# A convolution with max pooling: eight row sums moved to accumulating DMA, two more steps row-transformed, and the order written anew

## The chip, the cores and the metric

The kernel runs on one core of one Trainium2 chip. The metric is the device time of one execution in microseconds (us). The engines are named as in the profile: PE is TensorE (matrix products), PEld its loading of weights, DVE is VectorE, ACT is ScalarE, POOL is GpSimd, SP is SyncE, which here only issues transfers. Each engine works through its own list of instructions in order. It waits on semaphores for what other engines or transfers have to deliver, and whatever stands behind a waiting instruction on its list waits too.

## What is computed

A 3 x 3 convolution with zero padding over 16 images of 64 x 64 pixels and 64 channels, to 128 channels, and then the maximum over each 2 x 2 block of pixels:

```python
batch, c_in, h, w, c_out, k = 16, 64, 64, 64, 128, 3
x_pad = np.pad(x, ((0, 0), (0, 0), (1, 1), (1, 1)))
conv[b, co] += weight[co, ci, kh, kw] * x_pad[b, ci, kh:kh+h, kw:kw+w]   # over ci, kh, kw
output[b, co, i, j] = np.max(conv[b, co, 2*i:2*i+2, 2*j:2*j+2])
```

x, weight and the output are float32; the products are made in bfloat16 and summed in float32.

## The kernel before, in words

**Tiling.** Two images lie in the 128 partitions at a time (64 channels each), so there are eight pairs of images. A pair is cut into four quarters of 16 rows. One quarter of one pair is a step; there are 32 steps, 0 to 31. A step makes 8 rows of output for each of its two images, and its products run in two lanes, one per image (h = 0 or 1), each of which contracts over 64 partitions. Every product is three instructions (one per column of the 3 x 3 window) over 8 rows of 64 columns, at line 200. Products of the two lanes are issued in turn, so that two run at once.

**Two kinds of steps.** The string TYPES says of each step whether it is of kind K or W. Both need only sums and differences of the two rows that the pooling joins.

- A K step loads its rows as bfloat16 by a casting transfer from GpSimd's queue (`kload`, L95, tile `kx`), and adds each even row to the odd row after it on VectorE (KS, L298, tile `ks`). It makes five products per lane: PA1, PA2, PB1, PB2 and PR. That is 30 product instructions per step.
- A W step loads its rows as float32 by SP's queue (`wload`, L106, tile `wx`, of which there are three, each for a whole pair). From `wx` it makes three bfloat16 operands by row: E, the difference within each pair of rows (L329, tile `we`, 128 x 512); D, the differences to the rows above and below (L338, tile `wd`, 128 x 1024, always on GpSimd); and WS, the sum within each pair of rows (tile `ws`, 128 x 512). It makes four products per lane: P2 on `we`, P0 and P3 on `wd`, P1 on `ws`. That is 24 product instructions per step.

E runs on GpSimd, or on VectorE for the steps in DIFF_ON_VECTOR. WS runs on VectorE in one of two forms: a reduction (L312, for the steps in SUM_BY_REDUCTION) or a plain addition (L320). A GpSimd operation on SBUF is made to wait for the latest VectorE operation of that kind that stands ahead of it in the order (`behind`); the reductions are not counted among these.

**After the products.** Each lane of a step has two accumulators, a and b, out of eight banks of PSUM. EV on ScalarE copies a out to SBUF (L396, or L398 with a change of sign in a W step). In a W step, SE on ScalarE also copies a into b as a start (L408). MX on VectorE takes the larger of b and the copy (L424); the last product is then added to b; OD on ScalarE copies the odd columns out (L428); CM on VectorE takes the larger of even and odd columns (L434), and the result is stored through SP (L444; half of the last step through ScalarE's queue).

**Order.** All is written out by hand in one list, ORDER, with no scheduler behind it. An entry such as `P2.14.1` is product P2 of step 14 in lane 1, `L.14` the load of step 14, `LK.1.0` a load for K steps, `E.14`, `D.14`, `WS.14` the operands. The place of an entry sets its place on its engine. An entry of a product is issued only when the other lane has one too. At the start the weights are combined (D2, D0, GM, GP), turned by TensorE (T...) and copied out (V...), and the first steps of either kind run in halves (F and G). The pairs of images are given out to the K steps first, and then to the W steps.

Before, 11 steps are K and 21 are W; four E are on VectorE and 16 on GpSimd (the first W step makes its own in halves, L350 and L365); 11 WS are reductions and 10 plain additions.

Of the kernel before, what the change touches and what calls it, by code (L numbers as in the profile page):

```python
# [11 lines left out]
def kernel(  # L12
# [21 lines left out]
    R = HO // NQ  # L34


    TYPES = "KWKWWKWKWWKWWKWKWWKWWKWWWWKWWKWW"
    DIFF_ON_VECTOR = (3, 4, 6, 11,)
    CAST_ON_VECTOR = ()
    SUM_BY_REDUCTION = (1, 3, 9, 11, 12, 14, 16, 17, 19, 20, 22,)  # L40
    N = len(TYPES)
    KSTEPS = [s for s in range(N) if TYPES[s] == "K"]
    WSTEPS = [s for s in range(N) if TYPES[s] == "W"]
# [3 lines left out]

    const = ctx.enter_context(tc.tile_pool(name="const", bufs=1))
    kx_pool = ctx.enter_context(tc.tile_pool(name="kx_pool", bufs=-(-NK // NQ)))
    d_pool = ctx.enter_context(tc.tile_pool(name="d_pool", bufs=5))  # L50
    e_pool = ctx.enter_context(tc.tile_pool(name="e_pool", bufs=5))
    ws_pool = ctx.enter_context(tc.tile_pool(name="ws_pool", bufs=5))
    ks_pool = ctx.enter_context(tc.tile_pool(name="ks_pool", bufs=4))
    ev_pool = ctx.enter_context(tc.tile_pool(name="ev_pool", bufs=7))
    od_pool = ctx.enter_context(tc.tile_pool(name="od_pool", bufs=6))
    o_pool = ctx.enter_context(tc.tile_pool(name="o_pool", bufs=6))
    psum = ctx.enter_context(tc.tile_pool(name="psum", bufs=1, space=bass.MemoryType.PSUM))

# [10 lines left out]
    def behind(inst, other):  # L69
        if other is not None:  # L70
            tc.add_manual_dep(inst.ins, other.ins.name, SYNC, reason="order")
# [231 lines left out]
    def wx_rows(s):  # L303
        p, q = place[s]
        return wx[p % NWX], 2 * R * q + 1

    def ws(s):
        row["ws", s] = ws_pool.tile([128, R, W], BF16, name="ws")
        t, f = wx_rows(s)
        if s in SUM_BY_REDUCTION:  # L310
            with nc.allow_low_precision("bf16 operand of TensorE, as the other row sums"):
                nc.vector.tensor_reduce(  # L312
                    out=row["ws", s],
                    in_=t[:, f : f + 2 * R, :].rearrange("p (r two) w -> p r w two", two=2),
                    axis=mybir.AxisListType.X,
                    op=ADD,
                )
            return
        on_vector(
            nc.vector.tensor_tensor(  # L320
                out=row["ws", s], in0=t[:, f : f + 2 * R : 2, :], in1=t[:, f + 1 : f + 2 * R : 2, :], op=ADD
            )
        )
# [62 lines left out]

    def late_load(s):
        behind(wload(s), sbuf_op[0])

    ev, od, ot, made = {}, {}, {}, {}  # L390

# [58 lines left out]
    def cast_more(first):  # L450
# [36 lines left out]
    for m in PRODUCTS:  # L487
        steps[m] = lambda s, h, m=m: product(m, s, h)

    ORDER = """  # L490
        D0 g2 g1 TD0 TG2 g0 D2 XEa PR.0.1 TD2 VG2 PA1.2.1 VD0 TG0 uG1 TG1 GS F.2.0 VD2 XOa LB.3 LB.4 LB.6
        LB.8 LB.9 GM VG0 F.3.0 XOb F.0.0 uGM F.1.0 VG1 F.0.1 TGM PA2.2.1 XEb LK.0.0 F.1.1 F.2.1 F.3.1 VGM GP
        Ea KS.0 Eb EV.0.1 G.0.0 EV.0.0 G.0.1 uGP P2.3.1 SEa.0 SEa.1 SEb.1 MX.0.1 Da Db TGP SEb.0 MX.0.0 VGP
        LK.0.1 X2 PR.0.0 G.1.0 X1 G.2.0 PB1.2.1 PB2.2.1 WS.1 G.2.1 G.1.1 L.11 P0.3.1 PA1.2.0 PA2.2.0 P3.3.1
        OD.0.0 OD.0.1 EV.1.0 KS.2 E.3 CM.0.1 EV.1.1 P1.1.1 D.3 CM.0.0 PR.2.1 PB1.2.0 P2.3.0 MX.1.0 PB2.2.0
        EV.2.1 P1.3.1 SE.3.1 EV.2.0 WS.3 MX.1.1 P1.1.0 SE.3.0 P0.3.0 MX.2.0 MX.2.1 EV.3.1 PR.2.0 EV.3.0 D.4
        MX.3.1 OD.2.0 PA1.5.1 OD.1.0 E.4 PA1.5.0 PA2.5.0 P3.3.0 OD.1.1 OD.2.1 L.12 L.14 PA2.5.1 OD.3.1
        P2.4.1 CM.1.1 CM.2.0 P2.4.0 CM.1.0 PA1.7.1 D.6 EV.5.0 CM.3.1 CM.2.1 MX.3.0 PA2.7.1 PB1.5.1 SE.4.0
        PA1.7.0 PA2.7.0 EV.5.1 SE.4.1 EV.7.0 PB2.5.1 P0.4.1 P0.4.0 P2.6.1 KS.7 E.6 P3.4.1 WS.4 WS.6 P1.3.0
        EV.4.0 PR.5.1 KS.5 WS.8 EV.7.1 P0.6.1 PB1.5.0 PB1.7.0 PB2.5.0 PB2.7.0 L.16 P1.4.1 EV.4.1 MX.5.1  # L500
        P3.4.0 OD.3.0 SE.6.1 MX.5.0 LK.1.0 LK.1.1 CM.3.0 MX.4.1 P3.6.1 OD.5.1 PB1.7.1 MX.7.0 PB2.7.1 PR.5.0
        OD.5.0 P2.6.0 EV.6.1 E.8 PR.7.0 MX.4.0 OD.4.1 OD.7.0 CM.5.1 D.8 P1.4.0 SE.6.0 OD.4.0 CM.5.0 E.9
        MX.6.1 CM.7.0 CM.4.0 P1.6.1 P2.8.0 CM.4.1 D.9 P2.8.1 SE.8.0 P0.6.0 P2.9.1 MX.7.1 P3.6.0 OD.6.1
        EV.6.0 P0.8.0 L.17 P3.8.0 SE.8.1 CM.6.1 PR.7.1 EV.8.0 OD.7.1 P0.8.1 MX.6.0 SE.9.1 E.11 MX.8.0 P1.6.0
        D.11 CM.7.1 P2.9.0 OD.6.0 EV.8.1 CM.6.0 WS.9 P3.8.1 P1.8.0 P0.9.1 PA1.10.1 SE.9.0 P2.11.0 OD.8.0
        L.19 L.20 P3.9.1 PA2.10.1 KS.10 EV.9.1 SE.11.0 P0.9.0 CM.8.0 E.14 P2.11.1 MX.9.1 P3.9.0 MX.8.1
        P0.11.0 EV.9.0 EV.10.1 MX.9.0 P1.9.1 D.14 E.12 P1.8.1 PA1.10.0 P3.11.0 PA2.10.0 SE.11.1 OD.9.1
        P1.9.0 P2.14.0 WS.11 CM.9.1 P0.11.1 P3.11.1 EV.11.0 EV.11.1 OD.8.1 OD.9.0 EV.10.0 P1.11.0 PA1.13.0
        PA1.13.1 MX.11.0 MX.11.1 PA2.13.1 D.12 L.22 L.23 PA2.13.0 P2.12.0 CM.8.1 CM.9.0 D.16 P1.11.1 EV.13.1
        P2.12.1 OD.11.0 SE.14.0 OD.11.1 PB1.10.1 WS.14 P0.14.0 CM.11.0 PB2.10.1 P3.14.0 CM.11.1 L.24 P0.12.0  # L510
        SE.12.1 P0.12.1 SE.12.0 P3.12.1 P3.12.0 EV.14.0 PB1.10.0 P2.14.1 WS.12 PB2.10.0 EV.13.0 MX.10.1
        EV.12.1 MX.14.0 E.16 EV.12.0 MX.12.1 PR.10.1 P1.14.0 MX.12.0 SE.14.1 OD.10.1 P1.12.0 PB1.13.1
        PA1.18.0 KS.15 KS.13 CM.10.1 P0.14.1 MX.10.0 OD.14.0 P3.14.1 CM.14.0 EV.14.1 P1.12.1 PR.10.0
        PB2.13.1 WS.16 MX.13.1 PA2.18.0 PA1.15.1 PA2.15.1 PR.13.1 OD.10.0 MX.14.1 PB1.13.0 OD.12.1 EV.18.0
        LK.2.0 P1.14.1 PB2.13.0 P2.16.0 CM.10.0 L.25 PA1.15.0 OD.12.0 EV.15.1 OD.13.1 CM.12.1 PA2.15.0
        SE.16.0 CM.13.1 P0.16.0 CM.12.0 L.27 L.28 P3.16.0 MX.13.0 P2.16.1 D.17 PR.13.0 PB1.15.0 PB1.15.1
        E.17 D.20 E.20 D.19 PB2.15.1 PB2.15.0 SE.16.1 EV.15.0 WS.17 P0.16.1 MX.15.1 P3.16.1 EV.16.0 OD.14.1
        PR.15.1 P2.17.1 MX.16.0 P1.16.0 EV.16.1 OD.13.0 MX.16.1 OD.15.1 SE.17.1 CM.14.1 P1.16.1 P2.20.1
        CM.13.0 CM.15.1 OD.16.0 PA1.21.0 P2.17.0 MX.15.0 P0.17.1 PR.15.0 E.23 E.19 CM.16.0 P3.17.1 OD.16.1
        CM.16.1 SE.20.1 EV.17.1 P0.20.1 P3.20.1 WS.20 PA2.21.0 P2.19.0 OD.15.0 SE.17.0 P3.17.0 EV.20.1  # L520
        MX.17.1 CM.15.0 P1.17.1 E.24 P0.17.0 WS.22 PA1.21.1 SE.19.0 P0.19.0 OD.17.1 EV.21.0 MX.20.1 CM.17.1
        D.22 EV.17.0 PA2.21.1 EV.21.1 EV.19.0 P3.19.0 P2.19.1 MX.17.0 KS.18 P2.23.0 P1.17.0 WS.19 P1.20.1
        PA1.18.1 P0.19.1 SE.19.1 MX.19.0 PB1.18.0 OD.17.0 OD.20.1 PA2.18.1 PB2.18.0 EV.19.1 P1.19.0 CM.20.1
        D.23 CM.17.0 MX.18.0 E.22 P3.19.1 PB1.18.1 SE.23.0 P2.20.0 EV.18.1 MX.19.1 PB2.18.1 PR.18.0 P1.19.1
        KS.21 OD.19.0 P0.23.0 SE.20.0 P2.22.1 CM.19.0 P0.20.0 L.30 PR.18.1 OD.18.0 OD.19.1 MX.18.1 PB1.21.1
        E.25 P3.20.0 CM.18.0 EV.23.0 EV.20.0 OD.18.1 PB2.21.1 P2.22.0 PB1.21.0 WS.24 CM.19.1 P0.22.1 P3.22.1
        SE.22.1 CM.18.1 MX.20.0 PB2.21.0 SE.22.0 MX.21.1 MX.21.0 P0.22.0 L.31 PR.21.1 EV.22.1 P2.23.1
        EV.22.0 P3.22.0 P1.20.0 OD.21.1 PR.21.0 D.28 MX.22.1 OD.20.0 P2.24.1 MX.22.0 P1.22.0 CM.21.1 P1.22.1
        SE.23.1 OD.21.0 OD.22.1 CM.20.0 OD.22.0 D.24 WS.23 P2.24.0 P3.23.0 P3.23.1 P0.23.1 CM.21.0 CM.22.1
        SE.24.0 P2.25.1 CM.22.0 SE.24.1 P0.24.0 MX.23.0 P3.24.0 P0.24.1 P2.25.0 EV.23.1 LK.2.1 EV.24.0  # L530
        P3.24.1 P1.23.1 E.27 MX.23.1 D.25 P1.23.0 SE.25.1 MX.24.0 P1.24.0 EV.24.1 WS.25 MX.24.1 P0.25.1 D.27
        SE.25.0 P3.25.1 P0.25.0 OD.23.1 OD.23.0 EV.25.1 P1.24.1 CM.23.1 MX.25.1 CM.23.0 E.28 OD.24.0 EV.25.0
        P3.25.0 OD.24.1 CM.24.1 P2.27.1 PA1.26.0 SE.27.1 PA2.26.0 MX.25.0 P1.25.1 CM.24.0 PA1.26.1 P0.27.1
        OD.25.1 P2.27.0 CM.25.1 P1.25.0 P2.28.1 EV.26.0 PB1.26.0 P0.27.0 P3.27.0 WS.28 PB2.26.0 SE.27.0
        OD.25.0 PA2.26.1 P3.27.1 WS.27 KS.26 WS.30 D.30 EV.27.1 CM.25.0 MX.27.1 P2.28.0 PA1.29.0 E.31 E.30
        SE.28.1 PA2.29.0 EV.26.1 EV.27.0 P0.28.1 PR.26.0 P3.28.1 EV.28.1 D.31 P0.28.0 P1.27.1 SE.28.0
        PB1.26.1 MX.26.0 PB2.26.1 OD.27.1 CM.27.1 MX.27.0 MX.28.1 OD.26.0 P3.28.0 P1.27.0 PA1.29.1 EV.28.0
        EV.29.0 PA2.29.1 P1.28.1 P2.30.0 EV.29.1 MX.26.1 OD.28.1 OD.27.0 PR.26.1 P1.28.0 OD.26.1 CM.26.0
        MX.28.0 SE.30.0 CM.28.1 PB1.29.0 P0.30.0 P2.30.1 PB1.29.1 PB2.29.1 CM.26.1 CM.27.0 P0.30.1 SE.30.1
        P2.31.0 KS.29 OD.28.0 P3.30.0 CM.28.0 P2.31.1 EV.30.0 P3.30.1 SE.31.0 PB2.29.0 PR.29.1 MX.29.1 WS.31  # L540
        EV.30.1 P0.31.0 SE.31.1 MX.30.0 MX.29.0 EV.31.0 P0.31.1 P3.31.1 P3.31.0 PR.29.0 MX.30.1 MX.31.0
        EV.31.1 P1.30.1 OD.29.1 P1.30.0 MX.31.1 OD.29.0 P1.31.1 CM.29.0 CM.29.1 P1.31.0 OD.30.1 CM.30.1
        OD.30.0 OD.31.0 OD.31.1 CM.30.0 CM.31.0 CM.31.1
    """

    ones = nc.const_aps.tensor(1.0, [128, 512], BF16)
# [44 lines left out]
```

## Time and profile before

| | |
|---|---|
| median of 3 runs | 105.47 us (104.82 to 106.05) |
| profiled execution | 105.23 us |
| its span | 103.5 us |
| granted TensorE clock | 0.991 |
| bytes read from device memory, written to it | 17.14 MB, 8.39 MB |
| TensorE busy | 97.6 us |
| VectorE busy | 92.0 us |
| ScalarE busy | 82.2 us |
| GpSimd busy | 75.5 us |

The span is what the profile shows, from the first instruction to the last; the device time also holds what lies around it. A line of a group gives the line of the kernel, engine, operation, output and inputs, sizes and count; behind the bar the busy time, the mean duration of one in nanoseconds, and the idle time of the engine just before these instructions with what ended it. The busy time of TensorE counts overlapping products once. In the line of a transfer, the three numbers "to landing" are the shortest, median and longest time from issue until the data is there. In a line of a queue stand packets, MB written, and the time of its packets as a share of 16 DMA engines over the span.

### The profile page before, as it was taken

How to read it: one execution, taken by the hardware profiler on the slowest of the kernel's cores; microseconds unless marked ns; L12 is line 12 of the kernel's file. 1: busy time of each engine (PE TensorE's matmuls, PEld its weight loads, DVE VectorE, ACT ScalarE, POOL GpSimd, SP SyncE). 2: the span in 40 equal slices, each digit the busy share in tenths (PEclk: the TensorE clock that was granted, in tenths of full speed). 3: DMA queues.
4: the chain of work that ended last, by engine and by line, in shares of the span. 5: the costliest groups of instructions: out<-in, count | busy, mean ns of one | idle time of the engine just before them, and what ended most of it. 6: DMA issues, size and time to landing. Idle time of an engine off the chain costs nothing.

```text
span 103.5 us, 2545 instructions
## 1 busy us (share of the span) xinstructions
PE 97.6 (94%) x911; PEld 60.9 (59%) x911; DVE 92.0 (89%) x179; ACT 82.2 (79%) x181; POOL 75.5 (73%) x65
## 2 busy tenths in 40 slices
PE   6999999999999999999999999999999999999910
PEld 2496544555865565576666785556645777666500
DVE  1588899999999999999999999999989996979960
ACT  4545988986789997993887898987899898698820
POOL 6138769773995899998999997959997919970000
PEclk9999999999999999999999999999999999999996
DMA  2999999999999999998869990197789232007152
GB/s 50 350 339 279 377 300 263 388 408 298 197 215 303 286 328 374 341 327 168 166 163 285 380 371 27 44 217 256 172 155 246 93 137 101 0 12 249 49 203 101
DMA packets 13341, 23.33 MB, mean 226 GB/s; under 512 B 1040, under 2 KB 9488, under 8 KB 13328
## 3 DMA queue, kind: packets, MB, share of 16 engines
q1 hardware_dynamic: 12320, 20.68, 60.1%
q0 software_dynamic: 864, 2.36, 13.8%
q8 instruction: 7, 0.11, 0.4%
q10 hardware_dynamic: 144, 0.13, 0.4%
q14 instruction: 6, 0.05, 0.1%
HBM read 17.14 MB, written 8.39 MB: 247 GB/s over the span
## 4 chain that ended last, share of the span: by engine, by line
PE 87%; DVE 4%; POOL 3%; issue 2%; DVEq 0%; POOLq 0%
PE acc L200 82%; PE acc L548 3%; POOL wd L365 2%; PE acc L164 1%; DVE o L434 1%; DVE acc L424 1%; DVE wt L181 1%; DVE kx L448 1%; DVE wq L464 0%; DVEq L586 0%; POOL wq L151 0%; POOL kx L95 0%; DVEq L434 0%; POOLq L365 0%
## 5 line engine op out<-in xcount | busy, mean ns | idle before, releaser
L200 PEld LDWEIGHTS <-wt 64*128 64x128 bf16 x876 | 57.5, 94 | 33.4 <-issue 1.0
L338 POOL TENSOR_TENSOR wd<-wx 128x1024 bf16<-128x1024 f32 x20 | 47.1, 2360 | 8.2 <-PE acc L200 3.4
L200 PE MATMUL acc<-wd,wt 64*128 64x504 bf16 (+3 forms) x264 | 50.1, 367 | 0.1
L200 PE MATMUL acc<-kx,wt 64*128 64x504 bf16 (+6 forms) x288 | 50.0, 356 | 0.0
L424 DVE TENSOR_TENSOR acc<-acc,ev 128x512 f32<-128x512 f32 x64 | 42.1, 692 | 1.3 <-PE acc L200 0.4
L200 PE MATMUL acc<-we,wt 64*128 64x512 bf16 (+2 forms) x132 | 31.7, 367 | 0.0
L200 PE MATMUL acc<-ws,wt 64*128 64x504 bf16 (+1 forms) x126 | 28.7, 377 | 0.1
L398 ACT ACTIVATE ev<-acc 128x512 f32<-128x512 f32 x42 | 25.0, 607 | 2.7 <-PE acc L200 2.3
L428 ACT COPY od<-acc 128x256 f32<-128x256 f32 x64 | 22.6, 379 | 5.8 <-PE acc L200 5.2
L434 DVE TENSOR_TENSOR o<-acc,od 128x256 f32<-128x256 f32 x64 | 24.6, 417 | 2.1 <-ACT od L428 1.9
L408 ACT COPY acc<-acc 128x512 f32<-128x512 f32 x40 | 23.0, 581 | 3.0 <-PE acc L200 1.7
L329 POOL TENSOR_TENSOR we<-wx 128x512 bf16<-128x512 f32 x16 | 20.2, 1274 | 3.3 <-DVE ws L320 2.4
L200 PE MATMUL acc<-ks,wt 64*128 64x504 bf16 (+1 forms) x66 | 16.5, 377 | 0.1
L312 DVE TENSOR_REDUCE ws<-wx 128x512 bf16<-128x1024 f32 x11 | 13.5, 1230 | 0.0
L396 ACT COPY ev<-acc 128x512 f32<-128x512 f32 x22 | 12.9, 594 | 0.5 <-PE acc L200 0.5
L320 DVE TENSOR_TENSOR ws<-wx 128x512 bf16<-128x512 f32 x10 | 7.0, 720 | 0.0
L298 DVE TENSOR_TENSOR ks<-kx 128x512 bf16<-128x512 bf16 x11 | 4.6, 429 | 0.5 <-ACT kx L455 0.5
L548 PE MATMUL acc<-const-bfloat16-1.0 128*128 128x512 bf16 x8 | 3.6, 625 | 0.8 <-PEq L572 0.8
L95 POOL DMA_DIRECT2D kx<-in_x_dram x6 | 3.5, 590 | 0.7 <-DVE kx L448 0.7
L151 POOL COPY wq<-wq 128x64 bf16<-128x64 bf16 x3 | 0.7, 242 | 3.7 <-ACT wq L459 2.5
L164 PEld LDWEIGHTS <-wq 128*128 128x128 bf16 x25 | 2.2, 126 | 1.4 <-issue 1.1
L462 DVE TENSOR_TENSOR wq<-wraw 128x192 bf16<-128x192 f32 x1 | 0.5, 500 | 2.6 <-DMA wraw<-in_weight_dram 2.6
(32 smaller groups left out, 25.1 us busy)
## 6 DMA issues: line engine op xcount, KB each, us to landing
out_dram<-o SPq DMA_DIRECT2D x31, 256.0 KB, 4.2
wx<-in_x_dram SPq DMA_DIRECT2D x10, 512.0 KB, 6.3
wx<-in_x_dram SPq DMA_DIRECT2D x5, 544.0 KB, 8.7
wx<-in_x_dram SPq DMA_DIRECT2D x5, 480.0 KB, 6.8
kx<-in_x_dram POOLq DMA_DIRECT2D x2, 528.0 KB, 7.8
ksecond<-in_x_dram SPq DMA_DIRECT2D x1, 512.0 KB, 6.3
kx<-in_x_dram POOLq DMA_DIRECT2D x2, 256.0 KB, 7.1
kx<-in_x_dram POOLq DMA_DIRECT2D x1, 496.0 KB, 12.6
```

Of the source, the lines that this page charges most:

```text
L200: nc.tensor.matmul(acc[t][:, i0:i1, o0:o1], wt[lo : lo + CI, tap_of(m0, kw, h), :], rows(lo, i0, i1, c0, c1), start=start and kw == 1, sto ...
L312: nc.vector.tensor_reduce(out=row["ws", s], in_=t[:, f : f + 2 * R, :].rearrange("p (r two) w -> p r w two", two=2), axis=mybir.AxisListTy ...
L320: nc.vector.tensor_tensor(out=row["ws", s], in0=t[:, f : f + 2 * R : 2, :], in1=t[:, f + 1 : f + 2 * R : 2, :], op=ADD)
L329: inst = (nc.vector if vector else nc.gpsimd).tensor_tensor(out=row["we", s], in0=t[:, f : f + 2 * R : 2, :], in1=t[:, f + 1 : f + 2 * R : ...
L338: nc.gpsimd.tensor_tensor(out=row["wd", s], in0=t[:, f + 1 : f + 1 + 2 * R, :], in1=t[:, f - 1 : f - 1 + 2 * R, :], op=SUB)
L396: nc.scalar.copy(out=ev[s, h], in_=acc[t])
L398: nc.scalar.mul(ev[s, h], acc[t], -1.0)
L408: nc.scalar.copy(out=acc[t], in_=acc[ta[s, h]])
L424: nc.vector.tensor_tensor(out=t, in0=t, in1=ev[s, h], op=MAX)
L428: nc.scalar.copy(out=od[s, h], in_=acc[tb[s, h]][:, :, 1::2])
L434: nc.vector.tensor_tensor(out=ot[s][:, h], in0=acc[t][:, :, 0::2], in1=od[s, h], op=MAX)
L548: nc.tensor.matmul(acc[n].rearrange("p a b -> p (a b)"), ones[:, 0:128], ones, start=True, stop=True, skip_group_check=True)
```

## The change

Two steps turn from K to W: 9 are K and 23 are W. Ten E are on VectorE and 12 on GpSimd. Eleven WS are reductions (for another choice of steps), four are plain additions, and the other eight, of the steps in the new list SUM_BY_DMA, are made in a new way:

1. LC: SP loads the 16 rows of the step a second time, as float32, into a tile of a new pool (`sum`, 128 x 1024, six buffers). 0.52 MB.
2. LA: GpSimd issues a transfer from device memory that adds the rows 1 to 15 onto rows 0 to 14 of that tile. It reads 0.49 MB of x. Each even row then holds the sum wanted; the odd rows hold sums that nobody reads.
3. WS: ScalarE copies the even rows to the bfloat16 tile `ws`.

LA waits for LC, and WS for LA. Pools change as well: `d_pool` 5 to 6, `ks_pool` 4 to 3, `od_pool` 6 to 5. ORDER is a new list throughout. The combining of the weights starts with other entries, and all steps are placed anew.

```diff
-    TYPES = "KWKWWKWKWWKWWKWKWWKWWKWWWWKWWKWW"
-    DIFF_ON_VECTOR = (3, 4, 6, 11,)
+    TYPES = "KWKWWKWKWWKWWKWWWWKWWWWWWWKWWKWW"
+    DIFF_ON_VECTOR = (3, 4, 9, 12, 14, 15, 16, 17, 19, 20,)
     CAST_ON_VECTOR = ()
-    SUM_BY_REDUCTION = (1, 3, 9, 11, 12, 14, 16, 17, 19, 20, 22,)
+    SUM_BY_REDUCTION = (1, 3, 4, 8, 11, 14, 16, 20, 25, 30, 31,)
+    SUM_BY_DMA = (9, 12, 15, 17, 19, 22, 24, 27,)
...
-    d_pool = ctx.enter_context(tc.tile_pool(name="d_pool", bufs=5))
+    d_pool = ctx.enter_context(tc.tile_pool(name="d_pool", bufs=6))
...
-    ks_pool = ctx.enter_context(tc.tile_pool(name="ks_pool", bufs=4))
+    ks_pool = ctx.enter_context(tc.tile_pool(name="ks_pool", bufs=3))
...
-    od_pool = ctx.enter_context(tc.tile_pool(name="od_pool", bufs=6))
+    od_pool = ctx.enter_context(tc.tile_pool(name="od_pool", bufs=5))
+    sum_pool = ctx.enter_context(tc.tile_pool(name="sum_pool", bufs=6))
...
     def ws(s):
         row["ws", s] = ws_pool.tile([128, R, W], BF16, name="ws")
+        if s in SUM_BY_DMA:
+            nc.scalar.copy(out=row["ws", s], in_=row["sum", s][:, ::2, :])
+            return
...
+    def sum_load(s):
+        p, q = place[s]
+        row["sum", s] = sum_pool.tile([128, 2 * R, W], FP32, name="sum")
+        nc.sync.dma_start(out=row["sum", s], in_=rows_of(p, 2 * R * q, 2 * R * (q + 1)))
+
+    def sum_add(s):
+        p, q = place[s]
+        nc.gpsimd.dma_start(
+            out=row["sum", s][:, 0 : 2 * R - 1, :], in_=rows_of(p, 2 * R * q + 1, 2 * R * (q + 1)), accum_op=ADD
+        )
...
-        "KS": ks, "WS": ws, "E": we, "D": wd, "L": wload, "LB": late_load, "LK": lk,
+        "KS": ks, "WS": ws, "E": we, "D": wd, "L": wload, "LB": late_load, "LC": sum_load, "LA": sum_add, "LK": lk,
```

Of the new ORDER, the entries of one such step among their neighbours, with most entries between them left out:

```
L.11 L.12 G.1.1 EV.1.1 G.2.1 LC.9 EV.1.0
...
KS.5 LA.9 LK.1.1 PB2.5.0
...
CM.4.1 P0.6.0 P3.6.0 P0.6.1 MX.7.1 E.12 LA.12 EV.7.0 D.9
...
MX.8.1 WS.9 CM.7.0
...
L.25 L.27 LA.22 OD.16.0
...
LA.27 E.25 P3.22.0
```

## The prediction

> **What bounds the kernel now.** I read the page first, then the chain of work that ended last.
>
> ```profile
> span 103.5 us, 2545 instructions
> PE 97.6 (94%) x911; PEld 60.9 (59%) x911; DVE 92.0 (89%) x179; ACT 82.2 (79%) x181; POOL 75.5 (73%) x65
> ```
>
> ```profile
> 11.72 0.03 issue
> 11.76 64.24 PE acc L200 x603
> 75.99 0.03 issue
> 76.02 20.42 PE acc L200 x186
> ```
>
> From 11.76 to 96.44 us the chain is nothing but the products of L200: TensorE never waits, so everything else is hidden, and only the number of products counts. The timeline of TensorE shows their pace (start, duration):
>
> ```profile
> 31.18 0.38 PE L200 MATMUL acc<-wd,wt 64*128 64x512 bf16 x1
> 31.20 0.38 PE L200 MATMUL acc<-we,wt 64*128 64x512 bf16 x1
> ...
> 32.48 0.38 PE L200 MATMUL acc<-ws,wt 64*128 64x512 bf16 x1
> 32.49 0.38 PE L200 MATMUL acc<-wd,wt 64*128 64x512 bf16 x1
> ```
>
> Two run side by side, one per half of the rows; six pairs start in 1.30 us, whatever is printed as duration. The whole stretch, 84.68 us for 399 pairs, makes 0.212 us a pair. I use that as a ruler: an entry of the order with n pairs ahead of it stands at 11.76 + (n - 18) x 0.212 us, as 18 were done at 11.76; the new order is read by the same ruler.
>
> The cover is thin. By stretches (VectorE, ScalarE and GpSimd busy are the third to fifth pairs; the last columns are clock, DMA share, GB/s written):
>
> ```profile
> 8.00:24.00 16.00, 15.82 (x172) 8.84 (x172) 14.93 (x29) 13.80 (x31) 11.95 (x10) 1.00 1.04 338
> 34.00:46.00 12.00, 12.00 (x114) 7.13 (x112) 12.00 (x20) 11.09 (x25) 11.59 (x7) 1.00 1.00 337
> 56.00:62.00 6.00, 6.00 (x59) 4.55 (x57) 6.00 (x12) 5.33 (x13) 6.00 (x5) 1.00 1.03 378
> 12.00:92.00 80.00, 79.97 (x754) 50.23 (x750) 76.83 (x145) 68.93 (x154) 68.42 (x41) 1.00 0.79 230
> ```
>
> Of 80 us, VectorE is busy 76.8, ScalarE 68.9, GpSimd 68.4, DMA 0.79. A DMA share of 1 alone does not prove a full queue, so I looked at landings of the half-MB load of L106, one issued in a busy stretch, one alone:
>
> ```profile
> L106 SPq DMA_DIRECT2D wx<-in_x_dram x1: 386/386/386, 36.4 to 36.4; - x1
> DMA to landing us min/median/max: 9.5/9.5/9.5
> ```
>
> ```profile
> L106 SPq DMA_DIRECT2D wx<-in_x_dram x1: 460/460/460, 66.5 to 66.5; - x1
> DMA to landing us min/median/max: 4.9/4.9/4.9
> ```
>
> At 36 us a load waits nearly 5 us behind others, at 337 GB/s. So the transfers do queue in the first half; today that costs nothing, as loads stand 14 us or more ahead of their first reader (L.11 at 13.0, E.11 at 32.1).
>
> ```profile
> q1 hardware_dynamic: 12320, 20.68, 60.1%
> q0 software_dynamic: 864, 2.36, 13.8%
> ```
>
> ```profile
> L338 POOL TENSOR_TENSOR wd<-wx 128x1024 bf16<-128x1024 f32 x20 | 47.1, 2360 | 8.2 <-PE acc L200 3.4
> L329 POOL TENSOR_TENSOR we<-wx 128x512 bf16<-128x512 f32 x16 | 20.2, 1274 | 3.3 <-DVE ws L320 2.4
> L95 POOL DMA_DIRECT2D kx<-in_x_dram x6 | 3.5, 590 | 0.7 <-DVE kx L448 0.7
> ```
>
> **The change, part by part.**
>
> *Two K steps become W steps.* A K step has 30 products, a W step 24: 12 fewer, six pairs, all on the chain: -1.30 us. One of two zero matmuls of the start goes too, off the chain.
>
> *VectorE.* Six plain sums (L320, 0.720) go, -4.3; six differences come (L329 on VectorE, 0.683), +4.1; two KS (0.429) go, -0.9. Reductions stay eleven. Together -1.1: 75.7 of the 78.7 us left. Cost nothing, hidden by TensorE as now; without that cover it is 1 us the good way.
>
> *ScalarE.* Eight casts from the sum tile: no such row, so bounds: 0.581 (L408, same size) to 0.631 (L455, a cast in SBUF), I take L455 as the nearest: +5.0. Four more seeds of the new W steps x 0.581: +2.3. 76.2 of 78.7 us, 97%. Its idle time now is mostly waiting for TensorE (L428 5.2, L398 2.3 us), which closes without cost as long as no wait is added. Each cast adds one, for the landing of its addition; behind it in line stand evacuations and seeds, so TensorE runs out of accumulators.
>
> *GpSimd.* +2 D (2.360), -4 E (1.274), -1 cast load and +8 additions to issue. An issue of q0 costs 0.590 in the row of L95 (0.54 to 0.70 there); an addition may cost that or, if it issues two reads, twice: 4.7 to 9.4; I take 4.7, the row itself. Sum +3.7: 72.2 of 78.7. Each issue waits until its plain copy has landed, and all D and E behind it wait too; P0 and P3 need those D.
>
> *SP.* Eight copies of 0.52 MB go into its in-order queue among the stores. From the seventh on, each also waits until a cast has freed a sum tile (six there). Issue time, 0.4 us each, is idle time of SP.
>
> *Transfers.* Added: 8 x 0.524 MB on q1, 8 x 0.492 MB read on q0. What a MB costs in a full stretch: 338 GB/s written at 8 to 24 us, to which the cast loads (1.02 MB read, half that written) add 32, so 370; 337; 378. Weighted by length 0.36 MB/us, with ends 0.337 and, from the best 2 us of the trace (429 at 20 to 22), 0.43. Now the demand. LC.22, the copy ahead of the addition LA.22, has 15.3 MB on SP's queue up to its own end (26 loads and copies with the weights, 11 stores). On q0 go 3.1 MB of cast loads and five additions, 2.5 MB. 20.9 MB / 0.36 = 58.1 us; transfers count from 2.6 us (the page's first slice has 50 GB/s, the next 350), and a landing is reported late: a lone 0.26 MB store lands 2.1 us after issue, of which its bytes explain 0.7, so +1.4. LC.22 lands at 62.1 us; LA.22 stands at 55.0. So GpSimd stops for some 7 us. Before it, by the same sum, LC.15 (13.4 MB) lands at 41.2 for 39.1, LC.17 (17.3) at 51.9 for 46.8. These are one lateness, not added up.
>
> How much reaches the end? GpSimd has from LA.22 on nine D (21.2), eight E (10.2), three additions and one load (2.4): 33.8 us. 62.1 + 33.8 = 95.9 us; the first product on the last D, P0.31, stands at 91.3. +4.6 us. If rates are 0.337 the landing is 66.0 and the end +8.5; at 0.43, 52.6, nothing is late. The break-even is an LC.22 at 57.5, 0.39 MB/us. I take 0.36, as the measured stretches lie there, and only single windows above 0.39.
>
> A page gives another rate: the Trainium skill, "DMA: Bandwidth & Descriptors", section Bandwidth, measured 425 GB/s for one load of 16 MB and 341 for 1 MB. By the first the 20.9 MB take 49 us, nothing is late and the time is 104; by the second 61 us, and it is 111. The trace's mixed loads and stores, 337 to 378, are nearer the second.
>
> *Start and tail.* The new first order brings TensorE, by the durations of the rows there, to the end of the first W step's products at about 13.2 us, as now (11.76 + 1.49), with one K product exchanged for another; six odd copies and six CM follow the last maximum in both. 0, within 0.3 either way.
>
> **Sum.** Profiled execution 105.23 (span 103.5; 1.73 around it) - 1.30 + 4.6 = 108.5 us. Its own time is 0.24 below the median 105.47 of the runs shown.
>
> **Rivals.**
> 1. *The transfers keep up: faster.* If mixed traffic runs at 0.39 MB/us or more, additions and copies land in their leads (LC to LA 8.3 to 14.7 us, LA to WS 9.6 to 18.5, by the ruler; cast loads now land after 5.9 to 12.6). Then 105.23 - 1.30 = 103.9. For it: 429 GB/s once, no reader waits for a load now. Against: landings of 7 to 11 us at mere 337 to 370.
> 2. *An addition moves twice its bytes.* It must read the sum tile as well as x: 0.98 MB instead of 0.49. LC.22 then has five more reads ahead, 2.5 MB / 0.36 = 6.8 us: 108.5 + 6.8 = 115.3. No accumulating transfer is in the trace; the cast loads take about what their bytes read do. The Trainium skill, "Collectives: The Full Stack", section on the bandwidth ceiling, says of the add in a reduce step that it is slow not for its arithmetic but because "the add needs two source reads"; by that page this rival would hold. No run here shows it yet.
> 3. *The gain is given back, no more.* Copies land in time at about 0.38, but ScalarE at 97% waits for single casts: three of eight additions late by half a microsecond, or LC.22 late by 1.5 us beyond slack, gives 105.2 to 105.5. For it: LA to WS has only 9.6 to 10.2 us for steps 9, 15, 22 and 27, and a cast load took 12.6 in traffic.
>
> **How the numbers follow.** Late copies, 105.7 to 112 (rate 0.38 to 0.337, ends above): 0.42. Twice the bytes, 111 to 117: 0.12. Given back, 104.4 to 106.5: 0.20. Keep up, 103.6 to 104.4: 0.26. Predicted is the likeliest, 108.5; its own range is 105.7 to 112. For 8 in 10: from 103.9, which cuts under half of the good case, to 114, which cuts half of the doubled one. A measurement of this kernel tells about 1% from no change; faster means under 104.4. Faster 0.25, nearly the whole good case; same 0.20, most of the third case; slower 0.55.
>
> **What would show it.** Right: L200 rows near 864 at the same pace; waits of GpSimd (queue or D) for the sum copy, several microseconds in 35 to 65 us; half-MB landings of 10 us and more up to 65 us; DMA share 1 until 75 us; idle TensorE from about 40 us. Rival 1: chain all L200 until about 95 us and landings under 9. Rival 2: q0's share above 35%, packets of the additions twice as long as the cast loads' per byte read. Rival 3: ScalarE waits at the cast line. I am wrong if TensorE idles for an evacuation while copies land in time, or if additions cost GpSimd much over 0.6 us each.

## The result and the profile after

The changed kernel takes 115.5 us (median of four runs, 115.04 to 115.56), the kernel before 105.45 (104.82 to 106.05): a ratio of 1.096, with an interval of 1.090 to 1.103. It is 10.0 us slower, where 108.5 was forecast with a range of 103.9 to 114. The profiled execution took 115.52 us. All medians and ratios from here on are of fast runs, those within 1.5% of the fastest of the same kernel.

The page of the changed kernel, first its span and engines, then the busy tenths of the transfer engines in 40 slices, then the queues:

```profile
span 113.7 us, 2559 instructions
PE 99.7 (88%) x898; PEld 56.4 (50%) x898; DVE 96.9 (85%) x177; ACT 86.7 (76%) x193; POOL 82.2 (72%) x70
...
DMA  3999999999999999999999999999999992234034
...
q1 hardware_dynamic: 13760, 25.92, 62.2%
q0 software_dynamic: 1872, 5.77, 26.6%
```

All four compute engines stand still more than before (TensorE is busy 88% instead of 94%). What is full now are the transfer engines, 0.9 and more from the second slice to the 33rd, until about 93 us. In the chain that ended last, the unbroken row of products begins only at 83 us, where it began at 11.76 before:

```profile
82.43 0.58 ACT acc L425
83.01 0.04 issue
83.05 23.60 PE acc L202 x216
```

By stretches of the changed kernel (as in the prediction: TensorE's busy time comes first, the last columns are clock, DMA share and GB/s):

```profile
20.00:35.00 15.00, 13.76 (x127) 7.28 (x125) 14.80 (x24) 11.02 (x25) 12.28 (x10) 1.00 1.05 337
35.00:50.00 15.00, 14.05 (x125) 7.56 (x122) 13.35 (x26) 12.49 (x28) 11.31 (x6) 1.00 1.06 315
50.00:65.00 15.00, 13.26 (x117) 6.47 (x113) 14.41 (x24) 12.15 (x29) 12.40 (x7) 1.00 1.05 361
65.00:80.00 15.00, 13.54 (x119) 7.69 (x115) 11.83 (x23) 12.82 (x30) 14.45 (x9) 1.00 1.06 306
```

TensorE idles 1 to 1.7 us in each 15, at full clock; there is no one place. The idle time shows only part of the loss, as a product that runs without one of the other lane beside it counts as busy too: TensorE ran 488 instructions in these 60 us, where the kernel with the plain copies alone (below) ran 562. At 0.212 us a pair that is some 8 us. The lateness shows at whoever waits for a transfer: GpSimd for the plain copy, VectorE for a store to free an output tile (engine, tile and line, what it waited for, total us, times, longest):

```profile
POOL sum L403 <- DMA sum<-in_x_dram: 7.2, 3, 2.5
DVE o L451 <- DMA out_dram<-o: 5.0, 3, 2.8
```

The page's groups and issues (the last number of an issue is the median from issue to landing):

```profile
L343 POOL TENSOR_TENSOR wd<-wx 128x1024 bf16<-128x1024 f32 x22 | 53.4, 2456 | 5.3 <-issue 3.1
L334 DVE TENSOR_TENSOR we<-wx 128x512 bf16<-128x512 f32 x10 | 11.4, 1150 | 0.0
L403 POOL DMA_DIRECT2D sum<-in_x_dram x8 | 8.1, 1015 | 8.6 <-DMA sum<-in_x_dram 7.2
L312 ACT CAST ws<-sum 128x512 bf16<-128x512 f32 x8 | 5.0, 630 | 0.0
...
out_dram<-o SPq DMA_DIRECT2D x31, 256.0 KB, 8.9
wx<-in_x_dram SPq DMA_DIRECT2D x11, 512.0 KB, 11.0
sum<-in_x_dram SPq DMA_DIRECT2D x8, 512.0 KB, 11.2
sum<-in_x_dram POOLq DMA_DIRECT2D x8, 480.0 KB, 8.7
```

An addition takes 1.015 us of GpSimd to issue, not 0.59. The eight casts on ScalarE cost what was forecast (0.630) and wait for nothing.

### The profile page after: what moved, and what is told of

It reads as the page before. It is cut to its first block, busy times and chain, and to the rows that moved or that the text cites. A ratio compares the mean times of both kernels' runs of the same rounds, so it can differ in the third digit from the quotient of the medians.

```text
span 113.7 us, 2559 instructions
## 1 busy us (share of the span) xinstructions
PE 99.7 (88%) x898; PEld 56.4 (50%) x898; DVE 96.9 (85%) x177; ACT 86.7 (76%) x193; POOL 82.2 (72%) x70
## 3 DMA queue, kind: packets, MB, share of 16 engines
q1 hardware_dynamic: 13760, 25.92, 62.2%
q0 software_dynamic: 1872, 5.77, 26.6%
HBM read 25.26 MB, written 8.39 MB: 296 GB/s over the span
## 5 line engine op out<-in xcount | busy, mean ns | idle before, releaser
L202 PEld LDWEIGHTS <-wt 64*128 64x128 bf16 x864 | 53.6, 94 | 48.0 <-issue 13.3
L202 PE MATMUL acc<-wd,wt 64*128 64x504 bf16 (+3 forms) x288 | 58.1, 368 | 2.5 <-ACT acc L437 1.6
L343 POOL TENSOR_TENSOR wd<-wx 128x1024 bf16<-128x1024 f32 x22 | 53.4, 2456 | 5.3 <-issue 3.1
L202 PE MATMUL acc<-kx,wt 64*128 64x504 bf16 (+5 forms) x240 | 39.3, 352 | 0.7 <-DVE o L451 0.6
L202 PE MATMUL acc<-ws,wt 64*128 64x512 bf16 (+1 forms) x138 | 34.5, 376 | 2.9 <-DVE acc L441 2.8
L202 PE MATMUL acc<-we,wt 64*128 64x512 bf16 (+3 forms) x144 | 33.8, 368 | 1.9 <-DVE o L451 1.9
L334 POOL TENSOR_TENSOR we<-wx 128x512 bf16<-128x512 f32 x12 | 15.4, 1299 | 1.6 <-PE acc L202 1.3
L403 POOL DMA_DIRECT2D sum<-in_x_dram x8 | 8.1, 1015 | 8.6 <-DMA sum<-in_x_dram 7.2
L202 PE MATMUL acc<-ks,wt 64*128 64x504 bf16 (+1 forms) x54 | 13.5, 376 | 0.4 <-DVE acc L441 0.4
L334 DVE TENSOR_TENSOR we<-wx 128x512 bf16<-128x512 f32 x10 | 11.4, 1150 | 0.0
L312 ACT CAST ws<-sum 128x512 bf16<-128x512 f32 x8 | 5.0, 630 | 0.0
```

Source lines behind the costliest of these rows:

```text
L202: nc.tensor.matmul(acc[t][:, i0:i1, o0:o1], wt[lo : lo + CI, tap_of(m0, kw, h), :], rows(lo, i0, i1, c0, c1), start=start and kw == 1, sto ...
L312: nc.scalar.copy(out=row["ws", s], in_=row["sum", s][:, ::2, :])
L334: inst = (nc.vector if vector else nc.gpsimd).tensor_tensor(out=row["we", s], in0=t[:, f : f + 2 * R : 2, :], in1=t[:, f + 1 : f + 2 * R : ...
L343: nc.gpsimd.tensor_tensor(out=row["wd", s], in0=t[:, f + 1 : f + 1 + 2 * R, :], in1=t[:, f - 1 : f - 1 + 2 * R, :], op=SUB)
L403: nc.gpsimd.dma_start(out=row["sum", s][:, 0 : 2 * R - 1, :], in_=rows_of(p, 2 * R * q + 1, 2 * R * (q + 1)), accum_op=ADD)
```

## The experiments

Each was timed beside the kernel before on the same chip (median 105.0 to 105.2 there); ratios are to it. The first three take the addition apart.

**Without the transfers of the sums.** LC and LA leave the order, and the cast reads the loaded row:

```diff
-            nc.scalar.copy(out=row["ws", s], in_=row["sum", s][:, ::2, :])
+            t, f = wx_rows(s)
+            nc.scalar.copy(out=row["ws", s], in_=t[:, f : f + 2 * R : 2, :])
```

> The changed kernel without its sixteen sum transfers: neither the plain copy nor the addition is issued, and ScalarE casts the even rows of the step's own tile instead (the odd rows are left out of eight sums). All else, the order too, stays. Theory (the transfers' traffic and what waits for it cost the 11 us that TensorE idles more): about 104.5 us, that is 105.2 less 1.3 for the products, with up to 0.9 lost in the new start. Rival (the new order, its start and its shift of differences to VectorE are the cost): above 108 us.

Measured: 106.5 us (1.014, 1.010 to 1.017). So most of the loss goes with the transfers. But the kernel before less the 1.30 us of products would be 103.8, and 2.7 us are missing that have nothing to do with the transfers of the sums. The timeline of TensorE in this kernel shows where (start, duration, and in brackets the idle time ahead and what ended it):

```profile
10.86 0.50 PE L201 MATMUL acc<-wd,wt 64*128 64x256 bf16 x6 [1.11 <-ACT acc L437]
12.47 0.50 PE L201 MATMUL acc<-wd,wt 64*128 64x256 bf16 x6 [0.78 <-ACT acc L437]
18.66 0.39 PE L201 MATMUL acc<-wd,wt 64*128 64x512 bf16 x1 [0.48 <-ACT acc L425]
```

Three waits for seeds of ScalarE (its copies of a into b) in the first 20 us make 2.4 us: the new order of the start is the worse one. In the changed kernel itself the same three make 2.0 us (0.79, 0.78 and 0.47). The kernel before has no bracket at all between 8 and 21 us.

**The plain copies alone.** LA leaves the order, LC stays (the eight sums lack their odd rows).

> The changed kernel without the eight adding transfers; the eight plain copies on SP's queue stay, and ScalarE casts from them (the odd rows are left out of eight sums). Theory by bytes alone: 4.2 of some 12 MB added traffic (if an addition moves its bytes twice) remain, so about 3 to 4 of 11 us: 107.5 to 108.5. Theory by waits of GpSimd: GpSimd no longer waits for a copy, so 105 to 106. If the new order is at fault: above 110.

Measured: 106.4 us (1.013, 1.010 to 1.016). Eight copies of 0.52 MB cost nothing that shows. Full transfer engines alone need not cost TensorE anything, as a stretch of this kernel shows (TensorE never idle, DMA share 1.05):

```profile
35.00:50.00 15.00, 15.00 (x141) 9.01 (x137) 14.88 (x29) 14.21 (x32) 11.82 (x6) 1.00 1.05 377
```

**The second transfer as a plain write.** One word goes (the sums lack their even rows):

```diff
-            out=row["sum", s][:, 0 : 2 * R - 1, :], in_=rows_of(p, 2 * R * q + 1, 2 * R * (q + 1)), accum_op=ADD
+            out=row["sum", s][:, 0 : 2 * R - 1, :], in_=rows_of(p, 2 * R * q + 1, 2 * R * (q + 1))
```

> The changed kernel with the adding transfer replaced by a plain one of the same size, from the same queue, with the same waits (eight sums are then wrong: only the odd row is kept). If an addition moves its bytes twice, 3.9 MB less pass the transfer engines: 3.9 / 0.36 = 11 us of transfer time, of which 5 to 8 reach the end: 107 to 110.5. If an addition costs what a plain write of its size does: 115, no change. Time of GpSimd per issue: 0.6 instead of 1.0 us if it issues two reads.

Measured: 108.5 us (1.032, 1.026 to 1.038). Same bytes of x, same waits, same places in the order, and 7 us less. The page of this kernel:

```profile
span 106.7 us, 2558 instructions
...
q1 hardware_dynamic: 13760, 25.92, 65.7%
q0 software_dynamic: 1360, 5.77, 19.5%
...
L403 POOL DMA_DIRECT2D sum<-in_x_dram x8 | 4.5, 558 | 4.2 <-DMA sum<-in_x_dram 4.2
```

By stretches, as above:

```profile
35.00:50.00 15.00, 14.69 (x133) 9.01 (x131) 13.65 (x27) 13.15 (x30) 11.67 (x7) 1.00 1.04 398
50.00:65.00 15.00, 14.33 (x128) 7.63 (x125) 14.96 (x27) 13.71 (x32) 12.60 (x10) 1.00 1.04 408
```

The engines are as full as in the changed kernel (1.04 against 1.06 and 1.05), but move 398 and 408 GB/s instead of 315 and 361, and TensorE loses less than half as much. A queue's share times the span is the time that its packets held all 16 engines. Here q0 held them 20.8 us, 10.4 of it for the five cast loads (q0's 9.9% of 104.9 us in the kernel with the copies alone): 1.3 us for a plain write. In the changed kernel it held them 30.2 us: 2.5 us for an addition of the same size, in 144 packets instead of 80. Both kernels read the same 25.26 MB from device memory. Such engine times are rough in traffic: the same 25.92 MB of q1 come out at 70.0 to 74.1 us in the kernels with all eight copies. The issue differs too: 1.015 us against 0.558.

**One pair on an idle chip.** Behind the last VectorE instruction of the kernel before stand a copy into a new tile and then, three times, an addition and a plain transfer of 0.49 MB, each waiting for the one ahead:

```diff
+    behind(nc.sync.dma_start(out=probe, in_=rows_of(0, 0, 2 * R)), last_cm[0])
+    for _ in range(3):
+        nc.gpsimd.dma_start(out=probe[:, 0 : 2 * R - 1, :], in_=rows_of(0, 1, 2 * R), accum_op=ADD)
+        nc.gpsimd.dma_start(out=probe[:, 0 : 2 * R - 1, :], in_=rows_of(0, 1, 2 * R))
```

> The kernel before with six transfers put behind its last VectorE instruction, on a chip that is otherwise done but for the last stores: three accumulating transfers and three plain ones of the same 0.49 MB, in turn on one tile, each waiting for the one ahead. The theory that an addition keeps the 16 transfer engines about twice as long (2.5 against 1.3 us for each in the queue rows so far) expects the additions to land at least 1 us later than the plain ones here too, and to hold the engines about 1.9 times as long. The rival, that an addition is dear only among other traffic (by contention for memory or because its packets wait), expects the two to land within 0.5 us of each other. The issue on GpSimd should be about 1.0 against 0.56 us in either case. The time itself says nothing: the probe stands at the end, and adds six waits in a row, some 25 to 35 us.

By stretches, from the issue of one to the issue of the next, addition and plain write in turn:

```profile
104.76:110.58 5.82, 0.00 (x0) 0.00 (x0) 0.00 (x0) 0.00 (x0) 0.91 (x1) 0.50 0.56 84
110.58:115.33 4.75, 0.00 (x0) 0.00 (x0) 0.00 (x0) 0.00 (x0) 0.56 (x1) 0.50 0.35 103
115.33:121.33 6.00, 0.00 (x0) 0.00 (x0) 0.00 (x0) 0.00 (x0) 0.88 (x1) 0.50 0.54 82
121.33:125.82 4.49, 0.00 (x0) 0.00 (x0) 0.00 (x0) 0.00 (x0) 0.56 (x2) 0.50 0.35 109
```

With nothing beside it, an addition takes 1.1 to 1.5 us longer, and holds the engines 0.56 x 5.82 = 3.3 us against 0.35 x 4.75 = 1.7: twice. So the doubled engine time does not come from contention.

**Two plain writes for each addition**, the second into a spare tile (both engine time and issue of an addition, without being one; the sums lack their even rows):

```diff
-            out=row["sum", s][:, 0 : 2 * R - 1, :], in_=rows_of(p, 2 * R * q + 1, 2 * R * (q + 1)), accum_op=ADD
+            out=row["sum", s][:, 0 : 2 * R - 1, :], in_=rows_of(p, 2 * R * q + 1, 2 * R * (q + 1))
         )
+        spare = spare_pool.tile([128, 2 * R, W], FP32, name="spare")
+        nc.gpsimd.dma_start(
+            out=spare[:, 0 : 2 * R - 1, :], in_=rows_of(p, 2 * R * q + 1, 2 * R * (q + 1))
+        )
```

> The changed kernel with each addition replaced by two plain transfers of the same 0.49 MB, one over the copy and one into a spare tile that nobody reads (the odd rows are so left out of eight sums). Two plain transfers hold the 16 engines 2 x 1.3 = 2.6 us against 2.5 for an addition, and take 2 x 0.56 = 1.12 us of GpSimd to issue against 1.0. The theory that an addition costs what it holds of the transfer engines expects the changed kernel's time again: 114 to 117. The theory that its cost is the issue on GpSimd expects the same, and the next kernel tells the two apart. A third, that an addition is dear in a way of its own (its landing, waits that only it makes), expects no more than twice what one plain write cost: 106.4 + 2 x 2.1 = 110.6 or less.

Measured: 117.2 us (1.116, 1.105 to 1.127; two runs, 116.4 and 118.0), 1.7 us more than the changed kernel and 0.2 above what was expected. So an addition costs no more than two plain writes of its size, and no further price of adding is needed to explain its time. (The expectation has the rows the wrong way round: the write over the copy leaves the even rows out.) The page:

```profile
span 116.2 us, 2567 instructions
...
q1 hardware_dynamic: 13760, 25.92, 60.2%
q0 software_dynamic: 2000, 9.70, 27.0%
...
L404 POOL DMA_DIRECT2D sum<-in_x_dram x8 | 4.5, 560 | 8.5 <-DMA sum<-in_x_dram 8.5
L408 POOL DMA_DIRECT2D spare<-in_x_dram x8 | 4.3, 539 | 0.0
```

**A plain write and a tiny one**: the spare transfer cut to 16 rows of 256 bytes.

```diff
+        nc.gpsimd.dma_start(out=spare[0:16, 0:1, :], in_=rows_of(p, 2 * R * q, 2 * R * q + 1)[0:16])
```

> As the kernel with two plain writes, but the second of each two moves 16 rows of 256 bytes alone: GpSimd issues twice, and the transfer engines get next to nothing more than with one plain write. The theory of filled transfer engines expects one plain write's time again: 108 to 109.5. The theory that the 0.46 us more of issue on GpSimd each (3.7 us in all, and what waits behind it) make the cost expects the changed kernel's time: 113 to 116.

Measured: 109.8 us (1.046, 1.040 to 1.052), 1.3 us above the plain write and slightly above the range that was expected of filled engines. The second issue cost 0.506 us of GpSimd each, 4.05 in all, a little more than the 3.65 of the additions. So of the 7.0 us some 1.3 go with the issue, and the rest, some 5.7, with the engine time; each time is known to about 0.6 us, so that this split is an estimate.

**Three additions only** (steps 22, 24, 27; the other five cast from the loaded row, which leaves their odd rows out):

```diff
+            src = row["sum", s][:, ::2, :] if s in (22, 24, 27) else t[:, f : f + 2 * R : 2, :]
```

> The changed kernel with copy and addition for steps 22, 24 and 27 alone; the five other sums are cast by ScalarE from the row as it was loaded (their odd rows are left out), so that nothing but the number of transfers differs from the changed kernel and from the one without any (106.5). If each addition costs its share, 106.5 + 3/8 x 9.0 = 109.9 (109 to 111). If the cost is that of the filled engines, five pairs of transfers fewer leave 5 x (1.3 + 2.5) = 19 us of them free, and the stores and loads come in time but for a stretch around 65 us: 106.5 to 108.

Measured: 107.4 us (1.022, 1.017 to 1.028). Less than the 109.9 of a fixed price each. That fits a cost that comes only where the engines are full: of its five stretches of 15 us from 20 to 95 us TensorE idled in this one alone:

```profile
65.00:80.00 15.00, 14.81 (x133) 9.30 (x131) 13.77 (x26) 14.23 (x33) 14.41 (x10) 1.00 1.06 329
```

Whether the five earlier additions would cost more each, by their place, was not run. The variants that keep the changed kernel's places, with q0's and q1's shares times the span as engine time:

| kernel | engine time us | device time us |
|---|---|---|
| no transfers of the sums | 75.3 | 106.5 |
| plain copies alone | 84.4 | 106.4 |
| three additions | 86.9 | 107.4 |
| plain second write | 90.9 | 108.5 |
| plain and tiny write | 91.9 | 109.8 |
| changed kernel | 101.0 | 115.5 |
| two plain writes | 101.3 | 117.2 |
| half the rows (below) | 111.0 | 119.1 |

Up to about 85 us of engine time the time stays at 106.5; from there to the changed kernel it grows by 9 for 16.

**Passed-on waits.** Two runs took one visible wait away each: `o_pool` from 6 to 10 buffers, so that VectorE need not wait for stores, and the two differences E.12 and E.19 as reductions, as they met GpSimd operations (see the last section).

> The changed kernel with ten tiles for results waiting to be stored in place of six (o_pool 6 to 10). VectorE waited 5.0 us in three places for a store to free such a tile. If these waits cost what they show: 111 to 112.5 us, and the 5.0 us are gone from its waits. If they only pass on a lateness of the transfer queues that has other ways to reach TensorE (the wait of GpSimd for the copies, the load of the next rows): 114 to 115.5.

> The changed kernel with the two differences that met a GpSimd operation (E of steps 12 and 19, 2.87 us each in place of 0.68) made by a reduction of 1.23 us, which did not stretch beside GpSimd in any run (the two steps get the sum in place of the difference). If the meetings are on the path: 2 x (2.87 - 1.23) = 3.3 us less, 112 us. If they are on the path only in part, as TensorE waited 0.80 and 1.34 us behind them: 113.3 to 114. If they hide behind the transfers: 115.

Measured: 113.8 us (1.087, 1.078 to 1.095) and 115.2 us (1.097, 1.089 to 1.106). The first takes off about 1.7 us of the 5.0 that it showed, the second about 0.3, which is within the noise. The waits in the list mostly pass on a lateness that stays when one of them goes.

**Half the rows.** If bytes are the cost, copy only the even rows and add only the odd ones, into a tile of half the size:

```diff
-        nc.sync.dma_start(out=row["sum", s], in_=rows_of(p, 2 * R * q, 2 * R * (q + 1)))
+        nc.sync.dma_start(out=row["sum", s], in_=rows_of(p, 2 * R * q, 2 * R * (q + 1))[:, ::2, :])
-            out=row["sum", s][:, 0 : 2 * R - 1, :], in_=rows_of(p, 2 * R * q + 1, 2 * R * (q + 1)), accum_op=ADD
+            out=row["sum", s], in_=rows_of(p, 2 * R * q, 2 * R * (q + 1))[:, 1::2, :], accum_op=ADD
```

> The changed kernel with copies of the even rows alone and additions of the odd rows alone onto them: half the bytes on both (2.1 MB and, if read twice, 4.2), all sums still made, but in runs of 256 bytes where there were 4 KB. If bytes count: 109 to 111 us, and the time of the queue of the additions halves. If runs count (eight times as many): 117 us or more, and its time goes up.

Measured: 119.1 us (1.133, 1.123 to 1.142), slower still. The page:

```profile
span 118.1 us, 2551 instructions
...
q0 software_dynamic: 9040, 3.93, 28.2%
...
L403 POOL DMA_DIRECT2D sum<-in_x_dram x8 | 14.6, 1826 | 8.1 <-DVE acc L441 4.2
```

Fewer bytes, but in 9040 packets instead of 1872, as each row of 256 bytes now stands alone; q0 holds the engines 33.3 us instead of 30.2, and the issue takes 1.8 us. The copies went apart as well: q1 took 20928 packets instead of 13760, and 77.7 us instead of 70.7, for fewer bytes.

**The start mended.** The kernel without transfers of the sums, with four entries of the start moved ahead:

```diff
-        ... G.0.0 TGP Da WS.1 F.3.0 F.3.1 VGP Eb SEa.1 SEa.0 G.1.0 X2 G.0.1 X1 ...
+        ... G.0.0 SEa.1 SEa.0 X2 X1 TGP Da WS.1 F.3.0 F.3.1 VGP Eb G.1.0 G.0.1 ...
```

> The changed order without sum transfers (as no_sum_transfers; the odd rows are left out of eight sums), and with the four entries SEa.1 SEa.0 X2 X1 moved up to right behind G.0.0. TensorE had three gaps in its first 20 us (1.11, 0.78, 0.48), the first because the seed waits for a zero matmul that stands behind other products, the second because the next seeds wait behind two casts. If that is where the new order loses: 106.5 - 1.9 = 104.6 us, the first two gaps gone. If the loss is spread over the rest of the order: 106 to 106.5.

Measured: 105.55 us (1.006, 1.003 to 1.009), 1.0 less. The first of the three gaps is gone, the two others stay. That confirms the place of this part of the loss, for one gap of three; 1.9 was expected for two. The two gaps that stay are 1.3 of the some 1.8 us by which this kernel is still above 103.8; the rest stays open.

**The sums elsewhere.** With the start mended further (PA1 of step 2 ahead of G.2.0 too), the eight sums on GpSimd (`ws_gpsimd`, an addition of the two rows of `wx`); or five there and three on VectorE; or two on GpSimd, three on VectorE and three by transfer:

```diff
+    def ws_gpsimd(s):
+        row["ws", s] = ws_pool.tile([128, R, W], BF16, name="ws")
+        t, f = wx_rows(s)
+        on_gpsimd(
+            nc.gpsimd.tensor_tensor(
+                out=row["ws", s], in0=t[:, f : f + 2 * R : 2, :], in1=t[:, f + 1 : f + 2 * R : 2, :], op=ADD
+            )
+        )
```

> The changed kernel with the eight sums as one GpSimd addition each instead of the two transfers and the cast, with the starting order mended (the four seeds and PA1 of step 2 ahead of what waited for them) and eight buffers for the sums. Nothing of the computation is left out. GpSimd gets 8 x 1.28 = 10.2 us on the 75.1 of the kernel without the sums' transfers: 85 of a span of 103. The theory that the changed kernel was slow by its transfers alone, and that its six pairs fewer of products are worth their 1.3 us where the sums come in time, expects 103.7 to 105.0. The rival, that no engine has room left for the eight sums and that they are on the path wherever they are put, expects 107 to 110: GpSimd late by some of the 10 us and VectorE's two-input instructions waiting for its turns.

> As the kernel with the sums on GpSimd, but five sums on GpSimd and three (steps 15, 24 and 27) as VectorE additions. Nothing of the computation is left out. GpSimd 75.1 + 6.4 = 81.5, VectorE 92.2 + 3 x 0.72 = 94.4 of some 103. If the sums have room, 103.7 to 105.0, as with all eight on GpSimd; if GpSimd is what is short, this one is faster than all eight there by 1 us or more; if VectorE is, slower.

> As the kernel with the sums split, but with two sums on GpSimd (9, 17), three on VectorE (12, 15, 19), and the last three (22, 24, 27) still by a plain copy and an accumulating transfer. Nothing of the computation is left out. Eight additions cost 9.0 us against leaving both transfers out, of which 7.0 by being additions. If the cost is that of filled transfer engines, three of them (16 engines for 3 x (1.3 + 2.5) = 11.4 us instead of 30) fit into the room that the transfers of the kernel before leave (its engines were busy some 90% until 75 us) with 1 to 2 us lost: 104.5 to 106.5. If each addition costs its share whatever the load, 3/8 of 9.0 = 3.4 us: 107 to 109.

Measured: 113.0 (1.076, 1.070 to 1.082), 112.3 (1.069, 1.064 to 1.074) and 114.8 us (1.094, 1.088 to 1.099). All three missed what I expected of them. Placed so in this order, the eight sums have no room on GpSimd and VectorE: the best is only 3.2 us ahead of the changed kernel, and some of that may be the mended start (1.0 in the kernel without the transfers). In the third, VectorE's sums stretched to nearly twice their 0.74 us:

```profile
L326 DVE TENSOR_TENSOR ws<-wx 128x512 bf16<-128x512 f32 x7 | 9.6, 1366 | 0.0
```

How much of these three is stretched instructions, and how much an order that was not made for them, stays open. No version beat the kernel before.

**GpSimd not held behind VectorE.** In the kernel before, the wait that puts each GpSimd operation behind VectorE's latest (`behind` in `on_gpsimd`) is left out, to see what it is for:

```diff
     def on_gpsimd(inst):
-        behind(inst, sbuf_op[0])
         return inst
```

> The kernel before, with GpSimd's operations no longer made to wait for the latest VectorE operation on SBUF (an order that the data do not need). Theory (a VectorE operation with two inputs in SBUF stands still while a GpSimd operation on SBUF runs): rows of L320, L329, L298 that now take 0.68 and 0.43 us take up to 2.9, and the time goes up by 2 to 8 us. Rival (the two run side by side; the 2.87 us rows of the changed kernel are waits for data): rows as now, and 105 us or a little less, as GpSimd waits less.

Measured: 127.0 us (1.210, 1.204 to 1.216), far more than the 2 to 8 us expected; its rows stand in the last section.

## Why the prediction was wrong

**The step that failed** is the term "+4.6 (late copies)": 20.9 MB at 0.36 MB/us, the additions counted by the bytes that they read of x. Two errors of opposite sign lay in it.

- *The rate was too low.* With plain writes in place of the additions the traffic between 35 and 65 us ran at 398 and 408 GB/s, where I had taken 0.36 MB/us from stretches of the kernel before. So those rates were not the limit. At a DMA share of 1 and more the runs show anything from 289 to 429 GB/s; what sets the rate of a mix was not taken apart. Plain transfers of the same bytes cost 2.1 us (108.5 against 106.4), not 4.6.
- *The addition was priced as a plain transfer.* It holds the engines 2.5 us, not 1.3, and GpSimd 1.015 us, not 0.59. That made 7.0 us. Rival 2 had this mechanism and its time, 115.3, with a chance of 0.12. That its time came so close is in part luck: it stood on the same +4.6, which was 2.5 too much, and put the start at nothing, which was 2.7 too little. Its sentence "the cast loads take about what their bytes read do" was used against it though a cast load reads no tile; and the kernel had no row of an accumulating transfer, so that nothing in the profile spoke against twice. The rule of the Trainium skill that I cited there ("Collectives: The Full Stack", section on the bandwidth ceiling: the add needs two source reads) agrees with the runs: 1.9 times in traffic, 2.0 times alone. That the second half goes to reading the tile was not seen itself; the bytes read from device memory did not double.

*The path* was another one, too. The forecast had GpSimd stand still for some 7 us at the addition of step 22, which stands at 55.0 us in its reckoning, and carry that to its last D, on which TensorE would wait. GpSimd's additions of steps 9, 15, 17 and 22 and its last D, from the timeline of the changed kernel:

```profile
27.72 0.91 POOL L403 DMA_DIRECT2D sum<-in_x_dram  x1 [2.35 <-DMA sum<-in_x_dram]
43.90 0.90 POOL L403 DMA_DIRECT2D sum<-in_x_dram  x1 [2.49 <-DMA sum<-in_x_dram]
55.99 0.89 POOL L403 DMA_DIRECT2D sum<-in_x_dram  x1 [2.40 <-DMA sum<-in_x_dram]
65.09 0.89 POOL L403 DMA_DIRECT2D sum<-in_x_dram  x1 [0.28 <-issue]
100.64 2.35 POOL L343 TENSOR_TENSOR wd<-wx 128x1024 bf16<-128x1024 f32 x1
```

It waited for the copies of steps 9, 15 and 17, not for that of step 22, which went out at 65.1 us. From 83.05 us to the end of its products TensorE waited for nothing, the last D (done at 103.0) included. The time was lost before, piece by piece, over the whole stretch in which the transfer engines were full.

**Start and tail, "0, within 0.3"**, failed too: the start lost 2.0 us in the changed kernel, 2.4 without the transfers of the sums, by three waits for seeds. I had added up durations of the rows up to the end of the first W step's products, and had not asked for each product which seed on ScalarE stands ahead of it, and behind what.

By the runs, taken one after the other, the sum reads: 105.1 - 1.3 (products, taken from the forecast; no run measures them alone) + 2.7 (the rest of the new order; the rows of the start show 2.4 of it, a run confirms 1.0) + 0 (copies) + 2.1 (second transfer, as a write) + 7.0 (that it adds) = 115.6.

**What held.** The products: 864 in L202, and where TensorE is fed they run at nearly the old pace (216 in 23.60 us from 83.05 on, 0.219 us a pair against 0.212). ScalarE's casts hid. GpSimd waited for the sum copy three times, 7.2 us, as the list of signs said, though the first ended at 27.7 us already, and TensorE idled 1.24 us between 20 and 35 us, where I had said from about 40. Half-MB loads landed after 11.0 us, and the DMA share stayed above 1 until 80 us and at 0.97 from there to 95, where I had said 75. And "I am wrong if additions cost GpSimd much over 0.6 us each" came true.

**Signs that misled.** For rival 2 I had named a share of q0 above 35%; it was 26.6%, and rival 2 held. The share is of a longer span, and I had not worked it out from packets. The other sign, packets twice as long per byte read as those of the cast loads, pointed the right way: the engine time per MB read was 5.0 us for additions (19.8 us for 3.93 MB) against 2.8 for the cast loads (10.4 us for 3.69 MB), 1.8 times.

## What to carry to other kernels

In these runs a transfer that adds is not one transfer but two in engine time, and nearly two in issue: ask what the transfer engines have left (share times span) before moving arithmetic to them, and count twice. Take the limit of a resource from a stretch that is known to be filled by the same kind of traffic, not from a busy stretch of a kernel that did not need more. And a new order is a change of its own: read its start entry by entry, as the kernel with the sums' transfers left out was still 1.4% slower than before.

## What the runs showed of the hardware

**Two-input operations of VectorE and GpSimd exclude each other.** In the changed kernel E.12 on VectorE met a D on GpSimd (timeline: start, duration):

```profile
28.90 2.67 POOL L343 TENSOR_TENSOR wd<-wx 128x1024 bf16<-128x1024 f32 x1
29.26 2.87 DVE L334 TENSOR_TENSOR we<-wx 128x512 bf16<-128x512 f32 x1
```

The difference takes 0.70 us when alone (the mean of this line without the sums' transfers); here it ends at 32.13, 0.56 us after the D, as if it had begun only then. Without the waits that hold GpSimd behind VectorE, in the kernel before, this is the rule (page):

```profile
L328 DVE TENSOR_TENSOR we<-wx 128x512 bf16<-128x512 f32 x4 | 12.7, 3182 | 0.0
L297 DVE TENSOR_TENSOR ks<-kx 128x512 bf16<-128x512 bf16 x11 | 12.2, 1118 | 0.5 <-ACT kx L454 0.5
L319 DVE TENSOR_TENSOR ws<-wx 128x512 bf16<-128x512 f32 x10 | 9.8, 998 | 0.0
```

0.683, 0.429 and 0.720 us became 3.2, 1.1 and 1.0, and 105.1 us became 127.0. The reductions, with one input, kept their 1.23 us in every run. The Trainium skill, "SBUF — State Buffer", section "Who interferes with whom", states both: an exclusive lock between the two engines for such pairs, and that reductions do not contend. The prediction had overlooked it: a GpSimd made late by a transfer meets VectorE where the order had kept them apart. Here the price was small: taking the two meetings away brought about 0.3 us, within the noise.

**Packets.** An addition of 0.49 MB went in 144 packets, a plain write in 80; with rows of 256 bytes apart, the same queue needed 9040 packets for eight additions of half the bytes and five cast loads, and took longer than with whole runs.
